# Attention of a hybrid block: head weights half a head ahead, casts of the gated unit's weights behind named exponentials, quotients in halves

## The chip, the cores and the metric

The kernel runs on one core of one Trainium2 chip. The metric is the device time of one execution in microseconds, taken as the median of several runs. A profiled execution of the kernel before, with its trace, serves for the reading.

## The reference

One decoder layer on 1024 tokens of width 1024, in float32. Two branches read the same normalised input `u`: a diagonal state-space branch and a forgetting attention with 8 heads of 64. They are gated and added, projected, and followed by a cross-attention into 256 memory tokens, a gated feed-forward layer and a final norm. Cut to the parts that matter here:

```python
proj = u @ w_in[l]
u_ssm, q, k, v, f_logit, gate_logits = jnp.split(proj, [...], axis=-1)
y_ssm = gelu(s5_ssm(u_ssm, ...))
glu_a, glu_b = jnp.split(y_ssm @ w_glu[l], 2, axis=-1)
out_a = glu_a * sigmoid(glu_b)

# forgetting attention, per head, cum = cumsum(log_sigmoid(f_logit + b_forget))
s = (q @ k.T) * 64 ** -0.5 + cum[:, None] - cum[None, :]
s = where(causal, s, -inf)
att = softmax(s) @ v
out_b = att @ w_fox_o[l]

h = h + (gate_a * out_a + gate_b * out_b) @ w_mix_out[l]
...                      # cross-attention, gated feed-forward, final norm
```

## The kernel before

Products are made to float32's precision from two rounded halves: an operand is split into a high part (a cast on ScalarE, line 178) and a low part (a subtraction on VectorE, line 179), and each product is three matmuls (lines 168 to 170). Weights come through SP's DMA queue into tiles `raw` (two slots), and their halves lie in `whi` and `wlo` (four slots each).

The attention is the class `Fox`. Its loop `run` goes over the heads h = 0 to 7, and within a head over 12 units (qc, kt): a block of 512 queries against a tile of 128 keys, 4 units for the first block of queries and 8 for the second. For a unit, `scores` makes two matmuls (lines 1620 and 1621), adds the causal mask on VectorE (1623), takes the exponential on ScalarE (1627) and splits it into `ph` and `pl`; in four of the units the cast is on VectorE (1629, kept as `self.mark`) and the subtraction on GpSimd (1630), else on ScalarE and VectorE (1632, 1633). `values_hi` follows two units later (1645, 1646), `values_lo` one more unit later (1652). The last exponential that has been written down is `self.exp`.

Beside the units of head h the lists `side[i]`, one for each unit, hold work for later heads:

- the row maxima of head h + 1 (`row_max`, lines 1593 to 1598), turned into one row by `max_row` (1605 to 1610), which a DMA puts into the score operand `hb`;
- the projection of q and k of head h + 2: `parts` (16 steps of three matmuls), and `evac`, which writes the score operands and calls `gate_rows` for the rows of cumulated logs (1575, 1576);
- the split of the weights of head h + 3 at unit 9, and their load at unit 5 (1540, 1541), which is queued behind `self.spread`;
- in head 6 the loads of y, the gated unit's input (1698), into tiles that the normalised input leaves; in head 7 the loads of the finished heads (1704) and `filler`, the value half of the gated unit for its first four column blocks: for each a load with its split (`Glu.load`) and two products (`Glu.value`, each 12 matmuls and a copy on VectorE, line 1087).

When a head's last values are done, `finish` fetches the row of sums over a DMA, takes the reciprocal, writes it out (1665) and spreads it over 64 rows with a third DMA (1667, `self.spread`). `divide` of the head before runs at unit 4: it multiplies the 64 rows (1673), splits the product with lines 178 and 179 into `ahi` and `alo`, and stores both (1679; the last two heads go straight into the operand of the output projection, 1684).

The order in which this is written is not the order on the engines. A planner goes through all instructions with a model of their times and gives every engine and SP's queue a fixed order: it takes what is ready by its model, the one written first if several are, and a tile's slot must have been left by its last user. `tc.issue_after(ins)` binds the instructions that are written within it, and that belong to the engine of `ins`, to places behind `ins` in that engine's order; no wait comes of it. On the chip each engine goes through its list in order and waits at each instruction for what it needs. So a load of the gated unit's weights, written in head 7, can be issued in head 4, and its cast as well.

Of the kernel before, what the change touches and what calls it, by code (L numbers as in the profile page):

```python
# [10 lines left out]
F32R = mybir.dt.float32r  # L11
# [9 lines left out]
D = 1024  # L21
L = 1024
NT = 8
GRP = 32
NH = 8
DH = 64
# [40 lines left out]
def f32(ap):  # L67
    return ap.bitcast(F32)


class Act:


    def __init__(self, pool, tag, bufs, nk, n, kg=2, name="a"):
        self.kg, self.width = kg, D // kg

        def mk(s):
            return [[pool.tile([P, D], F32R, tag=tag, bufs=bufs, name=f"{name}{s}{k}_{h}")
                     .rearrange("p (k c) -> p k c", k=kg)
                     for h in range(n // self.width)] for k in range(nk // kg)]  # L80

        self.hi, self.lo = mk("h"), mk("l")
# [209 lines left out]
@with_exitstack  # L292
def hybrid_block_kernel(ctx: ExitStack, tc: tile.TileContext, x, mem, norm_mix, w_in, b_forget,
                        lam_re, lam_im, log_dt, b_re, b_im, c_re, c_im, d_skip, w_glu, w_fox_o,
                        w_mix_out, norm_mem_q, norm_mem_kv, w_mem_q, w_mem_kv, w_mem_o, norm_ffn,
                        w_ffn_in, w_ffn_out, norm_final, out):
    B = Block(ctx, tc)
    nc, V, A, G, T, S = B.nc, B.V, B.A, B.G, B.T, B.S
    small, const, ident = B.small, B.const, B.ident
    x, mem, out = x[0], mem[0], out[0]  # L300
    w_in, w_glu, w_fox_o, w_mix_out = w_in[0], w_glu[0], w_fox_o[0], w_mix_out[0]
    w_mem_q, w_mem_kv, w_mem_o = w_mem_q[0], w_mem_kv[0], w_mem_o[0]
    w_ffn_in, w_ffn_out = w_ffn_in[0], w_ffn_out[0]

    u_d = B.dram.tile([4, 8, P, P], F32, name="u_d")
    y_d = B.dram.tile([4, 2, 8, P, P], F32, name="y_d")
    gate_d = B.dram.tile([2 * D, L], F32, name="gate_d")
    att_d = B.dram.tile([2, NH * DH, L], F32, name="att_d")
    cum_d = B.dram.tile([NH, 2, L], F32, name="cum_d")
    rd_d = B.dram.tile([NH, L], F32, name="rd_d")  # L310
    kv_d = B.dram.tile([4, P, D], F32, name="kv_d")

    big = ctx.enter_context(tc.tile_pool(name="big", bufs=16))
    uT = Act(big, "big", 16, 8, L, name="u")
    with tc.tile_pool(name="ssm", bufs=1) as sp:
        s5 = S5(B, sp, lam_re[0], lam_im[0], log_dt[0], b_re[0], b_im[0], c_re[0], c_im[0], d_skip[0])
        with tc.tile_pool(name="xin", bufs=1) as xp:
            stage_in(B, xp, s5, x, mem, norm_mix[0], norm_mem_kv[0], w_in, w_mem_kv, uT, u_d, kv_d)
        with tc.tile_pool(name="qp", bufs=1, reuse_waits="tile") as qp:
            stage_ssm(B, s5, qp, uT, w_in, gate_d, u_d, y_d)  # L320
    yT = Act(big, "big", 16, 4, L, name="y")
    aT = Act(big, "big", 16, 4, L, name="at")
    sh = Shared(ctx.enter_context(tc.tile_pool(name="sh", bufs=1, reuse_waits="tile")))
    wg_d = B.dram.tile([4, P, 2 * D], F32, name="wg_d")
    glu = Glu(B, sh, yT, wg_d, gate_d)
    with tc.tile_pool(name="fox", bufs=1, reuse_waits="tile") as fp:
        Fox(B, fp, sh, uT, w_in, b_forget[0], cum_d, rd_d, att_d).run(y_d, yT, aT, w_glu, wg_d,
                                                                       [f for j in range(4) for f in glu.values(j)])
    with tc.tile_pool(name="st2", bufs=1, reuse_waits="tile") as s2:
        stage_tail(B, big, s2, sh, x, glu, aT, gate_d, kv_d, w_fox_o, w_mix_out, norm_mem_q[0], w_mem_q,  # L330
                   w_mem_o, norm_ffn[0], w_ffn_in, w_ffn_out, norm_final, out)
# [732 lines left out]
class Glu:  # L1064


    def __init__(self, B, sh, yT, w_glu, gate_d):
        self.B, self.sh, self.yT, self.w_glu, self.gate_d = B, sh, yT, w_glu, gate_d
        self.w, self.out = {}, {}

    def load(self, j):
        pieces = [(512 * i, (4, P), self.w_glu[:, :, i * D + j * P:i * D + (j + 1) * P].rearrange("k p c -> p k c"))
                  for i in range(2)]
        self.w[j] = [t[:, :D].rearrange("p (k c) -> p k c", k=8) for t in self.B.wload(pieces, D)]

    def product(self, j, h, b):
        ps = self.B.bank("mm" if b == 0 else None)
# [341 lines left out]
class Fox:  # L1419
# [247 lines left out]
        self.spread = S.dma_start(rb, self.rd_d[h].partition_broadcast(64))  # L1667
        self.rb[h] = rb

    def divide(self, h):  # L1670
        B, S = self.B, self.B.S
        num, rb = self.num.pop(h), self.rb.pop(h)
        B.V.tensor_mul(num[0:64, :], num[0:64, :], rb)
        hi = self.fp.tile([64, L], F32R, tag="rb", bufs=2, name="ahi")
        lo = self.fp.tile([64, L], F32R, tag="rb", bufs=2, name="alo")
        B.split(hi, lo, num[0:64, :])
        if h < NH - 2:
            for i, a in enumerate((hi, lo)):
                S.dma_start(self.att_d[i, h * DH:(h + 1) * DH, :], f32(a))
        else:  # L1680
            r = slice((h % 2) * DH, (h % 2 + 1) * DH)
            for hf in range(2):
                for dst, a in zip(self.aT.rhs(h // 2, hf), (hi, lo)):
                    S.dma_start(f32(dst[r, :]), f32(a[:, 512 * hf:512 * hf + 512]))

    def run(self, y_d, yT, aT, w_glu, w_d, filler):
        B, fp, S = self.B, self.fp, self.B.S
        self.aT = aT
        self.prepare_v()
# [5 lines left out]
        def load_y(k, h):  # L1695

            for i, dst in enumerate(yT.rhs(k, h)):
                S.dma_start(f32(dst).rearrange("p (t c) -> p t c", t=4),
                            y_d[k, i, 4 * h:4 * h + 4].rearrange("t p c -> p t c"))

        def load_att(k):
            for h in range(2):
                for i, dst in enumerate(aT.rhs(k, h)):
                    S.dma_start(f32(dst), self.att_d[i, k * P:(k + 1) * P, 512 * h:512 * h + 512])

        pro = [self.project(h) for h in range(NH)]
# [21 lines left out]
        pro[2].load()  # L1728
        pro[2].split(copied)
        pro[3].load()  # L1730
        for t in range(5, 7):
            self.values_of_v(0, t)
        units = [(qc, kt) for qc in range(2) for kt in range(4 * qc + 4)]
        for h in range(NH):
            side = {i: [] for i in range(12)}
            late = h == NH - 2
            if late:
                for i, f in enumerate(pro[h + 1].parts[8:]):
                    side[i // 2].append(f)
                side[3].append(pro[h + 1].evac[1])  # L1740
            if h + 1 < NH:
                for i, f in enumerate(self.row_max(h + 1)):
                    side[(RSLOT_LATE if late else RSLOT)[i]].append(f)
                side[9].append(lambda: self.max_row(h + 1))
            if h + 2 < NH:
                n = 8 if h + 3 == NH else 16
                for i, f in enumerate(pro[h + 2].parts[:n]):
                    side[i if n == 8 else PSLOT[i]].append(f)
                side[9].append(pro[h + 2].evac[0])
                if n == 16:  # L1750
                    side[11].append(pro[h + 2].evac[1])
            if h + 3 < NH:
                side[9].append(lambda: pro[h + 3].split(self.exp))
            if h > 0 and h + 3 < NH:
                side[5].append(lambda: pro[h + 3].load(self.spread))
            if h == 0:
                side[0].append(lambda: self.values_of_v(0, 7))
            if late:
                for k in range(8):
                    side[4 + k].append(lambda k=k: load_y(k // 2, k % 2))  # L1760
            if h == NH - 1:
                for k in range(3):
                    side[6 + k].append(lambda k=k: load_att(k))
                for i, f in enumerate(filler):
                    side[i * 12 // len(filler)].append(f)
            for i, u in enumerate(units):
                self.scores(h, *u)
                for f in side[i]:
                    f()
                if len(self.hi_todo) > 2:  # L1770
                    self.values_hi()
                if len(self.lo_todo) > 1:
                    self.values_lo()
                if h and i == 4:
                    with B.tc.issue_after(self.mark.ins):
                        self.divide(h - 1)
        while self.hi_todo:
            self.values_hi()
        while self.lo_todo:
            self.values_lo()  # L1780
        self.divide(NH - 1)


_INS = ["x", "mem", "norm_mix", "w_in", "b_forget", "lam_re", "lam_im", "log_dt", "b_re", "b_im", "c_re", "c_im",
# [26 lines left out]
```

## Time and profile before

| what | value |
|---|---|
| median of 3 runs | 1591.73 us (1591.47 to 1593.48) |
| profiled execution, span from its first to its last instruction | 1586.7 us |
| median of the runs less that span | 5.03 us |
| TensorE matmul busy, granted clock over the span | 1534.0 us (97%), 0.988 |
| weight load busy | 1261.3 us (79%) |
| VectorE, ScalarE, GpSimd busy | 1019.5, 655.2, 254.3 us |
| heads 1, 2, 3 (first exponential to the next head's) | about 24.75 us each |
| first exponential of head 4, of head 5, of head 6, of head 7 | 499.36, 529.83, 553.42, 579.40 us |

For the profiled execution the profile gives the span and no other time, so the span is what stands beside the runs. In the rows of the trace the first figure is the start in us from the span's start, the second the duration in us, then engine, line, operation and operands; in square brackets stands how long the engine was idle before it, and what ended the wait. `SPq` is the issue of a DMA on SP's queue, not its transfer. In rows of stretches each engine has its busy time with the count of instructions behind it.

### The profile page before, as it was taken

Reading aid. Unit: us, or ns where it says so; the run is one execution under the profiler, and the core shown is the slowest. Engines: PE = TensorE matmul, PEld = TensorE weight load, DVE = VectorE, ACT = ScalarE, POOL = GpSimd, SP = SyncE. Lnnn points to the kernel's source line nnn. Section 1 sums busy time; section 2 is a strip of 40 time slices with the busy share of each in tenths; the row PEclk is TensorE's granted clock in tenths of the full one; section 3 lists DMA queues with packets and bytes.
Section 4 is the critical chain, followed back from the end, with each engine's and each line's share of the span. In section 5 each row is a group of like instructions: output and inputs, shape, how many; then the busy total and the mean of one; then the engine's idle time right before and its main releaser. Section 6 shows DMA issues by size and latency. Waiting matters only on the chain.

```text
span 1586.7 us, 20446 instructions
## 1 busy us (share of the span) xinstructions
PE 1534.0 (97%) x7313; PEld 1261.3 (79%) x7313; DVE 1019.5 (64%) x1850; ACT 655.2 (41%) x1173; POOL 254.3 (16%) x335
## 2 busy tenths in 40 slices
PE   7799999999999899999999999999999999999997
PEld 6578888898777668888888778888888888788885
DVE  6666445344688687675555697766677776565555
ACT  6422434323576553222435564333333333254342
POOL 2027653200212124110002200100000000000001
PEclk8899999999999999999999999999999999999999
DMA  7764445652023736357412186555444554796642
GB/s 266 125 132 80 127 131 110 130 145 30 18 52 48 186 95 208 125 172 259 160 46 75 54 283 239 170 164 163 155 153 160 166 162 156 261 391 223 195 150 106
DMA packets 197940, 240.86 MB, mean 152 GB/s; under 512 B 35448, under 2 KB 126488, under 8 KB 197328
## 3 DMA queue, kind: packets, MB, share of 16 engines
q1 hardware_dynamic: 191216, 223.84, 48.2%
q10 hardware_dynamic: 6624, 15.73, 2.6%
q8 instruction: 57, 0.93, 0.2%
q14 instruction: 43, 0.35, 0.1%
HBM read 165.60 MB, written 75.86 MB: 152 GB/s over the span
## 4 chain that ended last, share of the span: by engine, by line
PE 75%; DVE 8%; DMA 7%; issue 4%; POOL 3%; ACT 2%; SPq 1%; DVEq 0%; POOLq 0%; ACTq 0%
PE mm L868 14%; PE mm L168 7%; PE pv L868 7%; PE mm L170 7%; PE mm L169 7%; PE mm L1005 4%; PE sc L868 3%; PE sc L1005 3%; PE pv L1005 3%; PE sc L168 3%; PE sc L169 3%; PE sc L170 3%; DMA raw<-in_w_in_dram 2%; PE misc L1005 1%; PE pv L168 1%
## 5 line engine op out<-in xcount | busy, mean ns | idle before, releaser
L179 DVE TENSOR_TENSOR wlo<-raw,whi 128x1024 fp32r<-128x1024 f32 (+2 forms) x121 | 132.0, 1094 | 135.1 <-ACT whi L178 133.9
L178 ACT CAST whi<-raw 128x1024 fp32r<-128x1024 f32 (+2 forms) x124 | 116.1, 940 | 220.0 <-DMA raw<-in_w_ffn_in_dram 54.1
L168 PE MATMUL mm<-uh,whi 128*128 128x512 f32 x344 | 138.8, 404 | 2.8 <-ACT whi L178 2.7
L170 PE MATMUL mm<-uh,wlo 128*128 128x512 f32 x344 | 136.5, 397 | 1.7 <-DVE wlo L179 1.7
L169 PE MATMUL mm<-ul,whi 128*128 128x512 f32 x344 | 136.4, 396 | 0.0
L179 DVE TENSOR_TENSOR ol<-or,oh 128x1024 fp32r<-128x1024 f32 x73 | 89.3, 1224 | 71.6 <-ACT oh L178 70.3
L178 ACT CAST oh<-or 128x1024 fp32r<-128x1024 f32 x73 | 76.8, 1052 | 105.3 <-PE mm L1005 33.6
L900 POOL TENSOR_TENSOR g<-a,c 128x512 f32<-128x512 f32 x22 | 35.2, 1600 | 392.8 <-ACT a L899 373.9
L170 PEld LDWEIGHTS mm<-uh,wlo 128*128 128x128 f32 x344 | 65.7, 191 | 16.5 <-DVE wlo L179 3.1
L1630 POOL TENSOR_TENSOR pl<-pf,ph 128x512 fp32r<-128x512 f32 (+1 forms) x32 | 39.7, 1239 | 241.1 <-DVE ph L1629 196.1
L168 PEld LDWEIGHTS mm<-uh,whi 128*128 128x128 f32 x344 | 65.9, 192 | 15.5 <-ACT whi L178 3.2
L169 PEld LDWEIGHTS mm<-ul,whi 128*128 128x128 f32 x344 | 66.0, 192 | 11.3
L197 POOL TENSOR_TENSOR r<-ms,mhalf 128x1 f32<-128x1 f32 x26 | 15.1, 582 | 354.9 <-DVE ms L193 344.5
L1627 ACT ACTIVATE pf<-sc 128x512 f32<-128x512 f32 (+1 forms) x96 | 46.5, 490 | 46.3 <-DVE sc L1623 28.6
L868 PE MATMUL pv<-S3h,we 128*128 128x512 f32 x176 | 58.1, 389 | 0.0
L1633 DVE TENSOR_TENSOR pl<-pf,ph 128x512 fp32r<-128x512 f32 (+2 forms) x64 | 35.1, 550 | 10.2 <-ACT ph L1632 9.5
L1005 PE MATMUL mm<-oh 128*128 128x512 f32 x106 | 41.2, 389 | 0.0
L1005 PE MATMUL mm<-ol,oh 128*128 128x512 f32 x106 | 41.2, 389 | 0.0
L1005 PE MATMUL mm<-oh,ol 128*128 128x512 f32 x106 | 41.2, 389 | 0.0
L168 PE MATMUL mm<-yh,whi 128*128 128x512 f32 x104 | 40.9, 393 | 0.0
L168 PE MATMUL sc<-uh,whi 128*128 128x512 f32 x104 | 40.8, 393 | 0.0
L170 PE MATMUL mm<-yh,wlo 128*128 128x512 f32 x104 | 40.6, 390 | 0.0
(580 smaller groups left out, 4537.5 us busy)
## 6 DMA issues: line engine op xcount, KB each, us to landing
or<-c_d SPq DMA_DIRECT2D x77, 256.0 KB
raw<-in_w_in_dram SPq DMA_DIRECT2D x22, 512.0 KB
wo<-in_w_ffn_out_dram SPq DMA_DIRECT2D x22, 512.0 KB
c_d<-g SPq DMA_DIRECT2D x44, 256.0 KB
t_d<-wo SPq DMA_DIRECT2D x44, 256.0 KB
or<-t_d SPq DMA_DIRECT2D x44, 256.0 KB
raw<-in_w_ffn_in_dram SPq DMA_DIRECT2D x20, 512.0 KB
rawb<-in_w_ffn_in_dram SPq DMA_DIRECT2D x20, 512.0 KB
```

The source lines that it names most:

```text
L168: T.matmul(ps, lh, rh, start=first, stop=False)
L169: T.matmul(ps, lh, rl, start=False, stop=False)
L170: T.matmul(ps, ll, rh, start=False, stop=last)
L178: self.A.copy(hi, src)
L179: (self.G if pool_lo else self.V).tensor_sub(lo, src, f32(hi))
L197: self.G.tensor_tensor(out=r, in0=v, in1=self.mhalf[:, 0:n], op=ALU.pow)
L868: T.matmul(ps, l_[:, k, :], r_, start=first and k == 0 and i == 0, stop=k == 3 and i == 2, skip_group_check=True)
L900: G.tensor_mul(g[:, 512:], a1, c1)
L1005: T.matmul(ps, l_[:, gi], r_[:, 512:], start=n < 3 and p == 0 and k == 0 or n == 7 and p == 0 and k == 0, stop=p == NP - 1 and k == 2, ski ...
L1627: self.exp = A.activation(pf[:, off:], ps[:, off:], AF.Exp)
L1630: G.tensor_sub(pl[:, off:], pf[:, off:], f32(ph[:, off:]))
L1633: V.tensor_sub(pl[:, off:], pf[:, off:], f32(ph[:, off:]))
```

## The change

Three things are changed, all in the attention.

- Head weights: the load of head h + 4 is written at unit 7 of head h (for head 0 too), where the load of head h + 3 was at unit 5 of heads 1 to 4. It is queued behind the spread of the head before, in head 0 behind an exponential. The splits stay at unit 9 for head h + 3.
- The gated unit's weights: the list of loads and products is moved one unit up: the first load stands at unit 10 of head 6, the other 11 steps at units 0 to 10 of head 7. The cast of each load is bound to come behind the exponential that was written last, on ScalarE's queue.
- `divide` is cut in two: at unit 4 the whole product and the split of the first 512 columns, at unit 6 the split of the second 512, bound behind that unit's exponential. The last two heads store each half as it is done, the others both at the end.

```diff
--- before.py
+++ after.py
@@ -324,8 +324,7 @@
     wg_d = B.dram.tile([4, P, 2 * D], F32, name="wg_d")
     glu = Glu(B, sh, yT, wg_d, gate_d)
     with tc.tile_pool(name="fox", bufs=1, reuse_waits="tile") as fp:
-        Fox(B, fp, sh, uT, w_in, b_forget[0], cum_d, rd_d, att_d).run(y_d, yT, aT, w_glu, wg_d,
-                                                                       [f for j in range(4) for f in glu.values(j)])
+        Fox(B, fp, sh, uT, w_in, b_forget[0], cum_d, rd_d, att_d).run(y_d, yT, aT, w_glu, wg_d, glu)
     with tc.tile_pool(name="st2", bufs=1, reuse_waits="tile") as s2:
         stage_tail(B, big, s2, sh, x, glu, aT, gate_d, kv_d, w_fox_o, w_mix_out, norm_mem_q[0], w_mem_q,
                    w_mem_o, norm_ffn[0], w_ffn_in, w_ffn_out, norm_final, out)
@@ -1067,11 +1066,12 @@
     def __init__(self, B, sh, yT, w_glu, gate_d):
         self.B, self.sh, self.yT, self.w_glu, self.gate_d = B, sh, yT, w_glu, gate_d
         self.w, self.out = {}, {}
+        self.after = None
 
     def load(self, j):
         pieces = [(512 * i, (4, P), self.w_glu[:, :, i * D + j * P:i * D + (j + 1) * P].rearrange("k p c -> p k c"))
                   for i in range(2)]
-        self.w[j] = [t[:, :D].rearrange("p (k c) -> p k c", k=8) for t in self.B.wload(pieces, D)]
+        self.w[j] = [t[:, :D].rearrange("p (k c) -> p k c", k=8) for t in self.B.wload(pieces, D, behind=self.after)]
 
     def product(self, j, h, b):
         ps = self.B.bank("mm" if b == 0 else None)
@@ -1667,23 +1667,23 @@
         self.spread = S.dma_start(rb, self.rd_d[h].partition_broadcast(64))
         self.rb[h] = rb
 
-    def divide(self, h):
+    def divide(self, h, hf):
         B, S = self.B, self.B.S
-        num, rb = self.num.pop(h), self.rb.pop(h)
-        B.V.tensor_mul(num[0:64, :], num[0:64, :], rb)
-        hi = self.fp.tile([64, L], F32R, tag="rb", bufs=2, name="ahi")
-        lo = self.fp.tile([64, L], F32R, tag="rb", bufs=2, name="alo")
-        B.split(hi, lo, num[0:64, :])
-        if h < NH - 2:
-            for i, a in enumerate((hi, lo)):
+        num = self.num[h]
+        cs = slice(512 * hf, 512 * hf + 512)
+        if hf == 0:
+            B.V.tensor_mul(num[0:64, :], num[0:64, :], self.rb.pop(h))
+            self.att = [self.fp.tile([64, L], F32R, tag="rb", bufs=2, name=n) for n in ("ahi", "alo")]
+        B.split(*[a[:, cs] for a in self.att], num[0:64, cs])
+        if h >= NH - 2:
+            r = slice((h % 2) * DH, (h % 2 + 1) * DH)
+            for dst, a in zip(self.aT.rhs(h // 2, hf), self.att):
+                S.dma_start(f32(dst[r, :]), f32(a[:, cs]))
+        elif hf:
+            for i, a in enumerate(self.att):
                 S.dma_start(self.att_d[i, h * DH:(h + 1) * DH, :], f32(a))
-        else:
-            r = slice((h % 2) * DH, (h % 2 + 1) * DH)
-            for hf in range(2):
-                for dst, a in zip(self.aT.rhs(h // 2, hf), (hi, lo)):
-                    S.dma_start(f32(dst[r, :]), f32(a[:, 512 * hf:512 * hf + 512]))
-
-    def run(self, y_d, yT, aT, w_glu, w_d, filler):
+
+    def run(self, y_d, yT, aT, w_glu, w_d, glu):
         B, fp, S = self.B, self.fp, self.B.S
         self.aT = aT
         self.prepare_v()
@@ -1728,6 +1728,13 @@
         pro[2].load()
         pro[2].split(copied)
         pro[3].load()
+        gated = [f for j in range(4) for f in glu.values(j)]
+
+        def behind_exp(f):
+            glu.after = self.exp
+            f()
+            glu.after = None
+
         for t in range(5, 7):
             self.values_of_v(0, t)
         units = [(qc, kt) for qc in range(2) for kt in range(4 * qc + 4)]
@@ -1751,18 +1758,19 @@
                     side[11].append(pro[h + 2].evac[1])
             if h + 3 < NH:
                 side[9].append(lambda: pro[h + 3].split(self.exp))
-            if h > 0 and h + 3 < NH:
-                side[5].append(lambda: pro[h + 3].load(self.spread))
+            if h + 4 < NH:
+                side[7].append(lambda: pro[h + 4].load(self.spread if h else self.exp))
             if h == 0:
                 side[0].append(lambda: self.values_of_v(0, 7))
             if late:
                 for k in range(8):
                     side[4 + k].append(lambda k=k: load_y(k // 2, k % 2))
+                side[10].append(lambda: behind_exp(gated[0]))
             if h == NH - 1:
                 for k in range(3):
                     side[6 + k].append(lambda k=k: load_att(k))
-                for i, f in enumerate(filler):
-                    side[i * 12 // len(filler)].append(f)
+                for i, f in enumerate(gated[1:]):
+                    side[i].append(lambda f=f: behind_exp(f))
             for i, u in enumerate(units):
                 self.scores(h, *u)
                 for f in side[i]:
@@ -1771,14 +1779,15 @@
                     self.values_hi()
                 if len(self.lo_todo) > 1:
                     self.values_lo()
-                if h and i == 4:
-                    with B.tc.issue_after(self.mark.ins):
-                        self.divide(h - 1)
+                if h and i in (4, 6):
+                    with B.tc.issue_after(self.mark.ins if i == 4 else self.exp.ins):
+                        self.divide(h - 1, i // 2 - 2)
         while self.hi_todo:
             self.values_hi()
         while self.lo_todo:
             self.values_lo()
-        self.divide(NH - 1)
+        for hf in range(2):
+            self.divide(NH - 1, hf)
 
 
 _INS = ["x", "mem", "norm_mix", "w_in", "b_forget", "lam_re", "lam_im", "log_dt", "b_re", "b_im", "c_re", "c_im",
```

## The prediction

> **What bounds the kernel now.** I read the page first, then each engine's busy time cut at the first exponential of each attention head, then the instructions of the heads in which TensorE stops.
>
> ```profile
> span 1586.7 us, 20446 instructions
> PE 1534.0 (97%) x7313; PEld 1261.3 (79%) x7313; DVE 1019.5 (64%) x1850; ACT 655.2 (41%) x1173; POOL 254.3 (16%) x335
> ```
>
> TensorE is busy for 97% of the span: only about 53 us of gaps exist, and the change touches only those of the attention heads. In the stretches below the columns are length, busy time and instructions of PE, PEld, DVE, ACT and POOL, then granted TensorE clock, DMA share and GB/s.
>
> ```profile
> 474.20:499.00 24.80, 24.76 (x122) 18.85 (x122) 20.27 (x51) 16.77 (x32) 4.60 (x4) 1.00 0.33 55
> 499.00:529.45 30.45, 26.95 (x122) 19.66 (x122) 21.34 (x51) 17.84 (x34) 4.60 (x4) 0.94 0.39 79
> 529.45:553.00 23.55, 21.52 (x107) 15.77 (x106) 18.48 (x51) 13.39 (x27) 4.62 (x4) 1.00 0.89 227
> 553.00:579.00 26.00, 22.66 (x107) 15.55 (x106) 22.15 (x48) 16.45 (x31) 6.37 (x4) 1.00 0.41 110
> 579.00:605.60 26.60, 26.52 (x129) 20.68 (x128) 17.34 (x29) 10.94 (x23) 4.63 (x4) 1.00 0.47 139
> 600.00:800.00 200.00, 200.00 (x901) 165.66 (x900) 131.65 (x173) 63.46 (x109) 31.60 (x22) 1.00 0.54 176
> ```
>
> These are heads 3 to 7 and the 200 us from 600 on. Head 3 is filled by TensorE (24.76 of 24.80 us). Head 4 has the same 122 matmuls and takes 30.45 us, 5.65 more: 3.50 is TensorE idle, 1.8 is clock (0.06 of 30.45), 0.3 I leave unplaced. Heads 5, 6 and 7 have 2.03, 3.34 and 0.08 us of idle. From 600 us TensorE has no gap, so I let what the heads save reach the end in full. All of it together is 5.65 + 2.03 + 3.34 + 0.08 = 11.1 us.
>
> **Head weights one head earlier.** Here is what stops head 4: ACT's casts, TensorE's wait, the clock after it, the DMA queue.
>
> ```profile
> 521.54 1.04 ACT L178 CAST whi<-raw 128x1024 fp32r<-128x1024 f32 x1 [4.85 <-DMA raw<-in_w_in_dram]
> 523.18 1.05 ACT L178 CAST whi<-raw 128x1024 fp32r<-128x1024 f32 x1 [0.18 <-DMA raw<-wg_d]
> 522.64 0.50 PE L168 MATMUL mm<-uh,whi 128*128 128x512 f32 x1 [2.74 <-ACT whi L178]
> 526.00:528.00 2.00, 2.00 (x8) 1.50 (x7) 1.70 (x4) 0.22 (x1) 0.00 (x0) 0.50 0.26 78
> 431.27 0.57 SPq L1540 DMA_DIRECT2D raw<-in_w_in_dram  x1
> 442.00:444.00 2.00, 2.00 (x11) 1.39 (x12) 1.97 (x5) 1.86 (x4) 0.40 (x1) 1.00 0.00 0
> 480.36 0.58 SPq L1540 DMA_DIRECT2D raw<-in_w_in_dram  x1
> 505.17 0.58 SPq L1540 DMA_DIRECT2D raw<-in_w_in_dram  x1
> 506.42 8.55 SPq L153 DMA_DIRECT2D raw<-wg_d  x2
> 508.00:510.00 2.00, 2.00 (x12) 1.50 (x11) 1.83 (x4) 0.93 (x2) 0.00 (x0) 1.00 0.45 26
> ```
>
> Head 1's load is issued at 431.27 and the DMA engines are empty by 442: about 10 us, and its cast comes later than that. In head 4 the load of head 7's weights (505.17) is followed at once by the first load of the gated unit's weights (506.42), whose issue holds SP's queue for 8.55 us while the engines move 26 GB/s. The head's weights are there only at 521.5, 16 us after their issue. ACT, in order, waits 4.85 us with the exponentials of units 10 and 11 behind it, and TensorE waits 2.74 us, then runs at half clock (0.50).
>
> The change issues each of heads 4 to 7's loads behind the spread of the head before, where a load goes today, but for the next head. Head 7's goes out near 480.4 and its cast stays near 516: 36 us for a 10 us transfer. Neither slot of `raw` is then free for the gated unit until head 6's weights are split at about 494, so the two loads no longer meet. Head 4's extra load is issued in head 0, where nothing else is to be moved:
>
> ```profile
> 380.00:420.00 40.00, 40.00 (x220) 32.39 (x219) 26.16 (x71) 18.98 (x36) 4.62 (x4) 1.00 0.00 1
> ```
>
> Its pin to an exponential orders nothing, since `issue_after` binds only instructions of the named one's engine and the load is SP's; at 1 GB/s that costs 0. Value: head 4 becomes head 3, **-5.65 us**; at worst the wait goes and half returns, -2.8. The lost clock in it is a measured 1.8 us. The Trainium skill, "TensorE: Matmul & The Clock Gate", section "Why this matters for your kernels", asks for idle gaps above about 3 us before the clock drops; here a gap of 2.74 us was followed by 0.50, so the trace is stricter. By the page no clock would have been lost to this gap, and the term would be about -3.8.
>
> **Gated unit's first transfers, now ahead of the rows of maxima.** Their casts are pinned, not their transfers. The first one takes the slot that head 6's weights leave:
>
> ```profile
> 493.12 1.22 DVE L179 TENSOR_TENSOR wlo<-raw,whi 128x1024 fp32r<-128x1024 f32 x1
> 494.56 0.70 SPq L1610 DMA_DIRECT2D hb<-mr  x1
> 498.36 0.39 PE L1620 MATMUL sc<-hb 69*128 69x512 f32 x1
> 503.14 0.35 SPq L1665 DMA_DIRECT2D rd_d<-rc  x1
> 504.65 0.47 SPq L1667 DMA_DIRECT2D rb<-rd_d  x1
> 548.81 2.08 SPq L153 DMA_DIRECT2D raw<-wg_d  x4
> 550.00:552.00 2.00, 1.97 (x12) 1.43 (x13) 1.15 (x4) 1.27 (x4) 0.00 (x0) 1.00 0.95 277
> 552.00:554.00 2.00, 2.00 (x11) 1.52 (x9) 0.85 (x3) 0.58 (x2) 0.00 (x0) 1.00 0.86 241
> ```
>
> The subtraction ends at 494.34, and head 4's row of maxima is issued at 494.56 and needed at 498.36. Two issues of 2.08 / 4 = 0.52 us get in between, and 0.5 MB at about 260 GB/s is 2.0 us, beginning some 1.2 us after its issue: drained at 494.34 + 1.2 + 2.0 = 497.5. A small transfer takes 1.5 us (503.14 to 504.65, where the second waits for the first). So the row lands near 498, just in time; the same comes at the end of head 4 with the second transfer. Lower end 0, upper end as under the rivals; I take **+0.5 us** for both.
>
> **Head 5.** Its wait is of another kind:
>
> ```profile
> 541.53 1.22 DVE L1673 TENSOR_TENSOR num<-num,rb 64x1024 f32<-64x1024 f32 x1 [1.60 <-DMA rb<-rd_d]
> 544.50 0.39 PE L1620 MATMUL sc<-hb,hb 69*128 69x256 f32 x1 [1.51 <-ACT pf L1627]
> ```
>
> The reciprocals of head 4 come late behind the loads of y, which the change leaves alone, and the product that waits for them stays whole. **0**; ends -2.03 (all of the idle gone, as ACT waits half as long for the shorter subtraction) and +0.5.
>
> **Head 6: the casts leave, and so does the filler.**
>
> ```profile
> 555.28 1.05 ACT L178 CAST whi<-raw 128x1024 fp32r<-128x1024 f32 x1
> 556.79 0.39 PE L1645 MATMUL pv<-ph,vhi 128*65 128x384 f32 x1 [0.60 <-ACT ph L1632]
> 558.00 1.04 ACT L178 CAST whi<-raw 128x1024 fp32r<-128x1024 f32 x1
> 559.39 0.51 PE L1620 MATMUL sc<-hb 69*128 69x512 f32 x1 [0.45 <-ACT pf L1627]
> 553.00:579.00 26.00, 6.13 (x18) 3.38 (x18) 0.00 (x0) 0.00 (x0) 1.00 0.41 110
> 553.00:579.00 26.00, 3.53 (x9) 1.69 (x9) 0.00 (x0) 1.00 0.41 110
> 575.88 2.19 DVE L1087 COPY sg<-mm 128x512 f32<-128x512 f32 x2
> ```
>
> Two casts inside head 6 each cost TensorE a wait (0.60 and 0.45). But because the weights are split so early, 18 + 9 = 27 matmuls of the gated unit (the two rows by tile, those that read y's high and low parts) run in head 6 and fill it. At 200 us / 901 = 0.222 us each they are 6.0 us. After the change the first cast follows the exponential of unit 10, so most of them move to head 7. Head 6 keeps 22.66 - 6.0 = 16.7 us of TensorE work; VectorE keeps 22.15 - 3 x 1.22 - 2.19 = 16.3, and 1.22 for the one subtraction, 17.5. No shorter than 17.5, then: idle 0.9, a change of -2.5. Head 5 with nearly that VectorE work ran 23.55 - 18.48 = 5.1 us over it: 22.6, idle 5.9, **+2.6**. The middle, 20.05, has 3.4 of idle, as now: **0**. I take the middle because the first products can still start within the head, in the gap after unit 10.
>
> **Head 7.** Three casts (3 x 1.05 on ACT) and three subtractions (3 x 1.22 on VectorE) enter it. It has 26.52 us of TensorE work, with the moved products some 32, against ACT's 10.94 and VectorE's 17.34: room for all. Each cast stands ahead of an exponential's own cast on ACT, so a wait like head 6's is possible: 0 to 3 x 0.6 = 1.8; I take **+0.8**. The next transfer starts when a cast frees its slot and has three units to land; two pairs took until 554 from 548.81, 5 us.
>
> **Quotients in halves.** A 64x1024 cast and subtraction become two of half the width, and the second cast follows the exponential of unit 6, by when VectorE is done with the first. Heads 1 to 4 hide the few tenths behind TensorE's 24.8; the copy of the next quotient, which waits for the last subtraction to leave `num`, is not needed before the bank comes round a head later. **0**, ends -0.5 and +0.5.
>
> **Sum.** -5.65 + 0.5 + 0 + 0 + 0.8 + 0 = -4.35 us on the profiled execution's span: 1582.35. The median of the runs, 1591.73, stands 5.03 above that span; what lies around it does not change: **1587.4**.
>
> **Rivals.** *Given back in heads 6 and 7.* Head 4's gain comes, but the missing filler costs the 2.6 and the casts the 1.8: -5.65 + 0.5 + 2.6 + 1.8 = -0.75, time 1591.0. For it speaks that head 6 loses 6 us of independent work; against it that VectorE's own load falls from 22.15 to 17.5. Chance 0.18, and with it 0.03 that the planner again puts a gated transfer beside a head's load, or that other waits come up, and nothing moves (1591.7).
>
> *Slower: the row of maxima behind the gated transfer.* Place: SP's queue at the end of heads 3 and 4. If the transfer moves as it did after 506.42 (26 GB/s) rather than as after 548.81, the row lands many microseconds late; all 12 scores of the next head wait, and TensorE stops long enough for the clock to drop. The point is a delay above 498.36 - 494.56 - 1.5 = 2.3 us. Price: twice a stop like head 4's, 2 x 5.65, in place of the 0.5: 1587.4 - 0.5 + 11.3 = 1598.2. Against it: the slow case had another load of narrow rows ahead of it, the fast one had not. Chance 0.17. The Trainium skill, "DMA: Bandwidth & Descriptors", section "Queues, rings and completion order", says that an engine takes the descriptors of one ring in order, which is what this rival needs; no row of this trace has a row of maxima directly behind a gated load.
>
> **Numbers.** The forecast has 0.62; its own range is 1582 to 1590. The lower ends, -5.65 - 2.03 - 2.5 for heads 4 to 6 and 0 for the rest, give -10.2 and 1581.5. The upper ends without the slow rival end at 1591.0 + 0.5 + 0.5 = 1592.0; with one of its two stops and the forecast's other terms, 1592.6. To leave out no more than 2 in 10 I go to 1596, between one stop and two. What a measurement of this kernel can tell from no change is about 0.2%, 3.2 us. Faster by more: 0.56 (the forecast less the part above 1588.5); within: 0.24 (that part, the first rival, one stop); slower: 0.20.
>
> **What would show it.** Right: the stretch of head 4 shrinks to about 25 us with a clock of 1.00, and no cast waits for w_in. No gated matmul before head 6's unit 10, and all of the rest in head 7, longer than now by some 5 us. Wrong: a wait of TensorE for the score operands right at the start of head 4 or 5 (the slower rival), head 6 no shorter than 26 us less the moved 6, plus 2 or more of idle (the first rival), or a cast on ACT in head 7 that waits for wg_d. Gaps in the tail that the before kernel lacks would break the carrying over.

## The result: 0.44% slower

| kernel | median of the runs | ratio to the kernel before |
|---|---|---|
| before | 1591.91 us (1587.22 to 1593.48) | 1 |
| changed | 1599.53 us (1597.31 to 1600.83) | 1.0044 [1.0032, 1.0056] |

The forecast was 1587.4 us with a range up to 1596.0. The time lies above the range, on the other side, and not by the mechanism of the slower rival. The profiled execution of the changed kernel took 1597.31 us, 1.7 more than its span, so the 5.03 us that the prediction put around the span of before were mostly the spread between executions.

The page of the changed kernel, and its stretches between the first exponentials of heads 1 to 7, of the stage's end (616.56, the load of the sigmoid's table) and of what follows:

```profile
span 1595.6 us, 20478 instructions
PE 1536.5 (96%) x7313; PEld 1263.5 (79%) x7313; DVE 1022.5 (64%) x1858; ACT 656.1 (41%) x1181; POOL 253.7 (16%) x335
```
```profile
425.16:451.61 26.45, 25.48 (x124) 19.07 (x122) 21.02 (x53) 16.90 (x33) 5.51 (x4) 1.00 0.25 52
451.61:477.95 26.34, 25.17 (x121) 18.96 (x121) 20.88 (x54) 16.79 (x33) 5.52 (x4) 1.00 0.31 52
477.95:504.26 26.31, 24.73 (x117) 18.44 (x118) 20.62 (x52) 16.79 (x33) 5.52 (x4) 1.00 0.37 71
504.26:530.61 26.35, 25.67 (x127) 19.24 (x125) 21.09 (x53) 16.79 (x33) 5.52 (x4) 1.00 0.18 46
530.61:555.19 24.58, 20.78 (x101) 15.12 (x102) 18.40 (x49) 13.61 (x29) 4.59 (x4) 1.00 0.80 209
555.19:579.75 24.56, 19.30 (x83) 13.60 (x83) 18.17 (x45) 14.83 (x30) 4.60 (x4) 0.86 0.23 55
579.75:616.56 36.81, 34.64 (x161) 25.75 (x160) 23.91 (x35) 14.86 (x28) 4.99 (x4) 1.00 0.53 151
616.56:800.00 183.44, 183.44 (x815) 152.01 (x814) 120.67 (x157) 58.05 (x93) 29.17 (x21) 1.00 0.57 185
```

TensorE's busy time has grown by 2.5 us for the same number of matmuls. From the sigmoid's table to the end the changed kernel takes 979.0 us and the kernel before 980.5, so what the heads lose reaches the end. The same cuts in the kernels of the experiments give this table (us, one profiled execution each). The ratios are against runs of the kernel before on the same chip, whose median lay between 1590.6 and 1592.7 us.

| kernel | heads 1 to 3 | head 4 | head 5 | heads 6 and 7 | ratio of the medians |
|---|---|---|---|---|---|
| before | 75.7 | 30.5 | 23.6 | 52.8 | 1 |
| **changed** | **79.1** | **26.4** | **24.6** | **61.4** | **1.0044** |
| loads alone | 75.6 | 25.0 | 23.3 | 52.8 | 0.9971 |
| casts alone | 75.7 | 29.1 | 24.0 | 59.1 | 1.0030 |
| halves alone | 79.3 | 31.4 | 23.6 | 53.5 | 1.0036 |
| loads and casts | 75.6 | 24.7 | 25.4 | 59.1 | 1.0000 |
| loads, steps unbound | 75.7 | 25.0 | 24.1 | 53.1 | 0.9954 |
| loads, first cast at unit 6 | 75.7 | 24.7 | 23.7 | 56.3 | 0.9978 |
| loads, first cast alone bound | 75.7 | 24.7 | 23.9 | 55.5 | 0.9980 |
| loads, whole quotient at unit 6 | 75.7 | 25.1 | 25.4 | 52.0 | 0.9957 |
| quotient's casts in halves | 77.0 | 30.0 | 23.7 | 53.7 | 0.9996 |
| quotient's subtractions in halves | 76.2 | 32.4 | 24.2 | 52.1 | 1.0004 |

The changed kernel wins 4.1 us in head 4, loses 3.4 in heads 1 to 3, 1.0 in head 5 and 8.6 in heads 6 and 7: +8.9 us, as much as the two spans differ (1.5 us more ahead of head 1 and 1.5 less behind head 7 cancel). Heads 1, 2 and 3 of the kernel before last 26.1, 24.8 and 24.8 us; "about 24.75" in the table of the time before holds for heads 2 and 3 only. The 1.0 of head 5 is no more than two executions of one kernel differ there (24.1 and 25.1 us with the loads and the steps unbound). Two places carry the loss.

**Each head's start.** TensorE (first two rows) and ScalarE at the start of head 3:

```profile
477.41 0.22 PE L1593 MATMUL mm<-hb 68*128 68x128 f32 x1
478.60 0.38 PE L1620 MATMUL sc<-hb,hb 69*128 69x256 f32 x1 [0.97 <-ACT pf L1627]
477.35 0.58 ACT L1568 CAST hb<-mm 64x512 fp32r<-64x512 f32 x1
477.95 0.60 ACT L1627 ACTIVATE pf<-sc 128x512 f32<-128x512 f32 x1
```

The score of the third unit (256 columns) waits 0.97 us for the head's first exponential, which stands on ScalarE behind a cast of the score operands. Nothing else stands ahead of that score in TensorE's list; the next matmul starts at 478.82.

**Head 6.** TensorE, then what it waits for on VectorE and ScalarE, then the clock:

```profile
568.01 0.40 PE L1652 MATMUL pv<-pl,vhi 128*65 128x512 f32 x1
573.45 0.37 PE L1607 MATMUL misc<-ident,mc 128*8 128x128 f32 x1 [5.04 <-DVE mc L1605]
568.21 1.22 DVE L1675 TENSOR_TENSOR num<-num,rb 64x1024 f32<-64x1024 f32 x1 [1.45 <-DMA rb<-rd_d]
569.46 1.14 ACT L178 CAST ahi<-num 64x512 fp32r<-64x512 f32 x2 [3.54 <-DVE num L1675]
570.43 1.28 DVE L179 TENSOR_TENSOR alo<-num,ahi 64x512 fp32r<-64x512 f32 x2
573.25 0.15 DVE L1605 TENSOR_TENSOR mc<-mc 128x8 f32<-128x8 f32 x1
```
```profile
572.00:574.00 2.00, 0.50 (x2) 0.21 (x2) 1.47 (x7) 1.10 (x3) 0.00 (x0) 0.50 0.94 201
576.00:578.00 2.00, 2.00 (x8) 1.48 (x8) 1.73 (x4) 0.66 (x2) 0.00 (x0) 0.50 0.00 0
```

The transposition of head 7's row maxima (line 1607) waits 5.04 us for VectorE, which starts the quotient at 568.21, behind a wait of 1.45 us for the spread reciprocals, and does its halves in between; no other work stands ahead of line 1607 in TensorE's list. Then TensorE runs at half clock until about 579. In the kernel with the loads alone the same place is covered. Here are the last matmul ahead of the stop, the first of the gated unit, the transposition without any wait, and what VectorE does meanwhile:

```profile
563.04 0.40 PE L1652 MATMUL pv<-pl,vhi 128*65 128x512 f32 x1
563.37 0.50 PE L168 MATMUL mm<-yh,whi 128*128 128x512 f32 x1
...
566.90 0.27 PE L1607 MATMUL misc<-ident,mc 128*8 128x128 f32 x1
566.59 0.15 DVE L1605 TENSOR_TENSOR mc<-mc 128x8 f32<-128x8 f32 x1
```

From 563.37 to 566.90 fifteen matmuls of the gated unit stand in TensorE's list, 3.5 us; in the changed kernel's list none is left ahead of line 1607.

### The profile page after: what moved, and what is told of

Same layout as the page of the kernel before. It is cut to its first block, busy times and chain, and to the rows that moved or that the text cites. A ratio compares the mean times of both kernels' runs of the same rounds, so it can differ in the third digit from the quotient of the medians.

```text
span 1595.6 us, 20478 instructions
## 1 busy us (share of the span) xinstructions
PE 1536.5 (96%) x7313; PEld 1263.5 (79%) x7313; DVE 1022.5 (64%) x1858; ACT 656.1 (41%) x1181; POOL 253.7 (16%) x335
## 4 chain that ended last, share of the span: by engine, by line
PE 71%; DVE 11%; DMA 6%; issue 5%; ACT 4%; POOL 3%; SPq 1%; DVEq 0%; POOLq 0%; ACTq 0%
PE mm L867 14%; PE pv L867 7%; PE mm L170 6%; PE mm L168 6%; PE mm L169 6%; PE mm L1004 5%; PE sc L1004 4%; PE sc L867 3%; PE pv L1004 3%; PE sc L168 3%; PE sc L169 3%; PE sc L170 3%; DMA raw<-in_w_in_dram 2%; PE misc L1004 2%; PE pv L168 1%
```

## The experiments

### One part at a time

Each part of the change by itself on the kernel before, and two of them together. The edits are the parts of the diff shown above.

**Loads alone**

```diff
-            if h > 0 and h + 3 < NH:
-                side[5].append(lambda: pro[h + 3].load(self.spread))
+            if h + 4 < NH:
+                side[7].append(lambda: pro[h + 4].load(self.spread if h else self.exp))
```

> The kernel before with only the head weights loaded one head earlier. The planner's lists of TensorE, VectorE, ScalarE and GpSimd stay as before; only SP's list changes. Theory (the transfer behind the gated one is what stops head 4, and nothing else hangs on it): head 4 falls from 30.4 to about 24.8 us, no idle before the cast of head 7's weights, the other heads as before; 1591.9 - 5.6 = 1586.3. Rival (the early loads are what makes heads 1 to 4 of the changed kernel 1.5 us longer each, by their transfers): heads 2 and 3 at 26.3 us instead of 24.8 and no gain over the whole, 1591 or more.

1586.84 us, 0.9971 [0.9959, 0.9983]. Heads 4 to 7:

```profile
501.59:526.59 25.00, 24.97 (x124) 19.02 (x124) 21.50 (x52) 17.75 (x34) 4.60 (x4) 1.00 0.22 54
526.59:549.89 23.30, 21.34 (x106) 15.55 (x104) 18.20 (x51) 13.25 (x27) 4.62 (x4) 1.00 0.89 236
549.89:575.88 25.99, 22.67 (x106) 15.60 (x105) 22.37 (x48) 16.58 (x31) 6.35 (x4) 1.00 0.38 106
575.88:602.71 26.83, 26.75 (x129) 20.79 (x129) 17.06 (x28) 11.38 (x23) 4.62 (x4) 1.00 0.46 138
```

Head 4 is 25.00 us at full clock where it was 30.5: the stop is gone, and nothing is given back in heads 5 to 7. On TensorE, VectorE, ScalarE and GpSimd the planner's lists are those of before; only SP's differs.

**Casts alone**

```diff
-    ...run(y_d, yT, aT, w_glu, wg_d, [f for j in range(4) for f in glu.values(j)])
+    ...run(y_d, yT, aT, w_glu, wg_d, glu)
...
+                side[10].append(lambda: behind_exp(gated[0]))
...
-                for i, f in enumerate(filler):
-                    side[i * 12 // len(filler)].append(f)
+                for i, f in enumerate(gated[1:]):
+                    side[i].append(lambda f=f: behind_exp(f))
```

> The kernel before with only the gated unit's steps one unit up and its casts bound behind exponentials. Theory (the filler that leaves head 6 is what the 5 us wait there costs): head 4 keeps its 30 us stall, heads 1 to 3 stay at 24.8, head 6 gets a wait of TensorE for the row maxima of about 5 us with the clock at a half after it, and the products move to head 7: 4 to 8 us slower, 1596 to 1600. Rival (the wait in head 6 comes from the halves, which put the whole product and two subtractions ahead of the last row maxima on VectorE): no wait over 2 us in head 6, within 2 us of before, 1590 to 1594.

1596.15 us, 1.0030 [1.0018, 1.0042]. Heads 6 and 7 last 59.1 us instead of 52.8:

```profile
551.32:573.89 22.57, 18.71 (x78) 12.60 (x77) 18.53 (x44) 14.51 (x28) 4.59 (x4) 0.85 0.26 68
573.89:610.39 36.50, 34.22 (x159) 25.41 (x158) 23.56 (x33) 14.78 (x28) 4.62 (x4) 1.00 0.50 147
```

Head 6 has lost 28 matmuls, keeps 3.9 us of idle and runs at a mean clock of 0.85; head 7 has 30 more and is 9.7 us longer. The stop at line 1607 is 3.7 us here, where about 5 was expected.

**Halves alone**

```diff
-                if h and i == 4:
-                    with B.tc.issue_after(self.mark.ins):
-                        self.divide(h - 1)
+                if h and i in (4, 6):
+                    with B.tc.issue_after(self.mark.ins if i == 4 else self.exp.ins):
+                        self.divide(h - 1, i // 2 - 2)
```

> The kernel before with only the quotients split in halves. Theory (the halves turn the planner's order of heads 1 to 4 into one that leaves TensorE waiting): heads 2 and 3 at 26.3 us instead of 24.8, in all 5 to 6 us slower by heads 1 to 4, less what of head 4's stall the longer heads take up, so 1592 to 1598. Rival (the early loads do that): heads 2 and 3 stay at 24.8, within 2 us of before, 1590 to 1594.

1596.40 us, 1.0036 [1.0022, 1.0051]. Heads 2 and 3 last 26.33 and 26.30 us, 1.5 more than in the kernel before; head 1 is 0.5 longer and head 4, with its stop still there, 1.0. This is head 3:

```profile
476.48:502.78 26.30, 25.15 (x121) 18.96 (x121) 20.81 (x54) 16.79 (x33) 5.50 (x4) 1.00 0.30 52
```

**Loads and casts**, the change without the halves:

> The changed kernel without the halves. Theory: head 4 at 24.8, heads 2 and 3 at 24.8, the wait in head 6 stays: the loads' gain of 5.6 against the casts' loss of 4 to 8, 1590 to 1594. Rival (the halves make the wait in head 6): the wait is gone as well, 1586 or less.

1591.39 us, 1.0000 [0.9986, 1.0014]. The gain of the loads and the cost of the casts cancel. The single effects, -4.6, +4.8 and +5.7 us by the ratios, add to +5.9, and the whole change costs +7.0 (5.1 to 8.9): an effect of the parts on each other is not shown.

### Why the halves cost 1.5 us in heads 2 and 3

The place of the second half is not it. Written at unit 6 and bound to the mark instead of the exponential, it gets lists that are the same on all five queues; written at unit 4, lists that differ in the order of two stores of the last heads. So the cut is left. What was open was whether it is the time of the smaller instructions or the other order that the planner writes around them.

**Only the cast in halves**

```diff
-        B.split(hi, lo, num[0:64, :])
+        for hf in range(2):
+            cs = slice(512 * hf, 512 * hf + 512)
+            B.A.copy(hi[:, cs], num[0:64, cs])
+        B.V.tensor_sub(lo, num[0:64, :], f32(hi))
```

> The kernel before, with only ScalarE's cast of the quotient cut in two halves (ahi, line 178); VectorE's subtraction stays whole, in its old place. TensorE's list through heads 1 to 6 is that of before but for one place. Theory 'order': what costs about 1.5 us in each of heads 1 to 4 with halves of both is the other order in which the planner then writes the heads, not the extra instruction. Then heads 2 and 3 last 24.8 us here as before, and the whole is within 0.2% of before (1587.5 to 1593.5 us). Rival 'small instructions': two halves take longer than one whole (1.14 against 1.05 us on ScalarE, 1.62 against 1.22 us on VectorE), and this delays the exponentials that follow on the same engine. Then heads 2 and 3 are longer here too, by a share of the 1.5 us, some 0.3 us each.

**Only the subtraction in halves**

```diff
-        B.split(hi, lo, num[0:64, :])
+        B.A.copy(hi, num[0:64, :])
+        for hf in range(2):
+            cs = slice(512 * hf, 512 * hf + 512)
+            B.V.tensor_sub(lo[:, cs], num[0:64, cs], f32(hi[:, cs]))
```

> The kernel before, with only VectorE's subtraction of the quotient cut in two halves (alo, line 179); the cast stays whole. TensorE's list departs from that of before from head 1 on. Theory 'order': heads 1 to 4 then leave 24.8 us, most likely for about 26.3 us as with halves of both, and the whole is 1595 to 1597 us. Rival 'small instructions': 0.4 us more on VectorE in each head, which has 4 us idle in each, so that heads 2 and 3 become longer by 0 to 0.4 us, and the whole is 1590 to 1593 us.

1590.87 us, 0.9996 [0.9985, 1.0006], and 1593.09 us, 1.0004 [0.9995, 1.0014]. Head 2 with the casts in halves, then with the subtractions:

```profile
454.08:478.89 24.81, 24.77 (x123) 18.87 (x123) 20.23 (x51) 16.86 (x34) 4.61 (x4) 1.00 0.27 55
```
```profile
451.30:476.39 25.09, 25.08 (x122) 18.83 (x121) 20.01 (x52) 16.38 (x32) 4.64 (x4) 1.00 0.28 54
```

Neither theory came through whole. The casts alone cost heads 2 and 3 nothing, as "order" said; TensorE's list through heads 1 to 4 is that of before. The subtractions alone change TensorE's list from head 1 on and cost 0.3 us a head, which is what "small instructions" allowed and not the 1.5 that "order" expected. So another order is not dear in every case. But the two together cost 1.5, so 1.2 us of it appears with neither cut alone.

The traces show what is different in the list with both cuts. The quotient's two casts still run back to back, at the place of the whole one in ScalarE's list, so the cut spreads nothing. On VectorE the planner puts a step in writing the score operands of a later head (line 1564) behind the quotient's subtractions, 16.2 us into head 2, where it stood ahead of them, at 11.5 us. The later steps of these operands follow late, and head 3's first exponential stands on ScalarE behind the last of them. TensorE's first score, on the other hand, comes 3.4 us ahead of that exponential (at 476.48) instead of 1.0 (at 476.80). Here is the halves alone, TensorE at the start of head 3, then VectorE in head 2; then the same rows of the loads alone:

```profile
473.07 0.40 PE L1620 MATMUL sc<-hb,hb 69*128 69x512 f32 x1
477.13 0.39 PE L1620 MATMUL sc<-hb,hb 69*128 69x256 f32 x1 [0.96 <-ACT pf L1627]
462.83 1.62 DVE L179 TENSOR_TENSOR alo<-num,ahi 64x512 fp32r<-64x512 f32 x2
466.35 0.68 DVE L1564 SCALAR_TENSOR_TENSOR hb<-mm,hb 64x512 fp32r<-64x512 f32 x1
```
```profile
475.80 0.40 PE L1620 MATMUL sc<-hb,hb 69*128 69x512 f32 x1
477.45 0.39 PE L1620 MATMUL sc<-hb,hb 69*128 69x256 f32 x1
463.51 0.68 DVE L1564 SCALAR_TENSOR_TENSOR hb<-mm,hb 64x512 fp32r<-64x512 f32 x1
464.22 1.22 DVE L179 TENSOR_TENSOR alo<-num,ahi 64x1024 fp32r<-64x1024 f32 x1
```

This chain and its wait of 0.96 us are read from the traces; no run isolated them, so that the order is the cause is argued, and some 0.5 of the 1.5 us is left unplaced. Head 1 with the casts in halves, 27.4 us against 26.1, has a stop of its own (1.24 us on TensorE) and shows that even the smaller cut is not free everywhere.

**The whole quotient at unit 6**, on top of the loads:

```diff
-                if h and i == 4:
+                if h and i == 6:
```

> Head weights loaded earlier; the quotient whole, written at unit 6 in place of unit 4. TensorE's list is that of the loads alone through heads 1 to 5, with 17 matmuls of the gated unit ahead of line 1607 in place of 15. Theory 'the cut, not the place': heads 2 and 3 last 24.8 us, and the whole is that of the loads alone within 0.2% (1584 to 1589 us). Rival 'the place': the later quotient takes VectorE and ScalarE where the exponentials need them, heads 1 to 4 go to 26 us as with the halves, and the whole is 1591 us or more.

1587.11 us, 0.9957 [0.9942, 0.9972]; head 2 lasts 24.86 us. The later place of the whole quotient costs nothing; the cut does.

### Why the casts cost 6 us in heads 6 and 7

**Steps one unit up, casts not bound**

```diff
         def behind_exp(f):
-            glu.after = self.exp
+            glu.after = None
             f()
```

> Head weights loaded earlier and the gated unit's steps written one unit up, as in the kernel with both parts (1591.4 us), but the casts of the gated unit's weights not bound behind exponentials. Theory 'binding': the binding holds the first cast back to unit 10 of head 6 and with it every product that could fill head 6. Without it 15 matmuls of the gated unit stand ahead of the transposition of head 7's row maxima on TensorE (line 1607) as in the kernel before, where the binding leaves none; the wait of 3.7 us there is gone, heads 6 and 7 together last 52.8 us where they lasted 59.1, and the whole is 1586 to 1588 us, as with the loads alone. Rival 'place': the loads written one unit up meet other transfers, and the cost stays: 1590 to 1592 us.

1585.25 us, 0.9954 [0.9941, 0.9966]; heads 6 and 7 last 53.1 us, without the wait at line 1607:

```profile
548.76:574.76 26.00, 22.63 (x106) 15.59 (x105) 22.37 (x48) 16.60 (x32) 6.36 (x4) 1.00 0.39 107
574.76:601.87 27.11, 26.94 (x130) 20.79 (x130) 16.95 (x28) 11.49 (x23) 4.61 (x4) 1.00 0.46 137
```

The binding is the cause, as its theory said. The place of the steps is nothing: with the first load written at unit 4, 6, 8 or 10 of head 6 and no binding, the lists are the same. Run once more beside the loads alone:

> Head weights loaded earlier and the gated unit's steps one unit up, the casts not bound. Theory 'no effect of the place': what the planner can move freely it puts where it was, 15 matmuls of the gated unit ahead of line 1607 in head 6 with the steps either way, so the time is that of the loads alone within 0.2% (3 us). Rival 'a gain of its own': the steps one unit up are worth the 1.6 us that lay between the two kernels in separate comparisons (1585.3 and 1586.8 us), and it lies 1 to 2 us below the loads alone here too.

> Head weights loaded earlier and nothing else, beside the kernel with the steps unbound. Both theories: 0.997 of before, some 4.6 us less.

1586.54 us, 0.9962 [0.9948, 0.9977], and 1586.48 us, 0.9965 [0.9952, 0.9978]. No gain of its own.

**First cast four units earlier, all bound**

```diff
-                side[10].append(lambda: behind_exp(gated[0]))
+                side[6].append(lambda: behind_exp(gated[0]))
```

> As the kernel with both parts (1591.4 us), all casts bound, but the first load written at unit 6 of head 6 in place of unit 10, so that its cast is bound behind the exponential of unit 6. Theory 'filler': it is the first cast alone that empties head 6. With it four units earlier 18 matmuls of the gated unit stand ahead of line 1607 in head 6, the wait of 3.7 us and the half clock behind it go, and heads 6 and 7 together last 53 to 55 us: 1585 to 1588 us. Rival 'all casts': the other three casts, bound to units 2, 5 and 8 of head 7, keep the products for the end of head 7, which stays near 36 us less what moved; heads 6 and 7 last 57 us or more and the whole 1589 to 1591 us.

1589.37 us, 0.9978 [0.9965, 0.9990]; heads 6 and 7 last 56.3 us, between both theories, and the whole lies where "all casts" had it. The wait at line 1607 is gone; what is left is in head 7, with waits of TensorE for the casts and subtractions of the gated unit. The list of its waits from 545 to 612 us (total, times, longest) has, among others:

```profile
PE mm L170 <- DVE wlo L179: 1.5, 2, 0.9
PE mm L168 <- ACT whi L178: 0.4, 1, 0.4
```

**First cast alone bound**

```diff
-                    side[i].append(lambda f=f: behind_exp(f))
+                    side[i].append(f)
```

> As the kernel with loads and casts (1591.4 us, heads 6 and 7 together 59.1 us), but only the first cast is bound, behind the exponential of unit 10 in head 6; the other three are free. With the first cast four units earlier and all four bound, heads 6 and 7 lasted 56.3 us; with none bound 53.1 us. Theory 'two halves': the first binding empties head 6 (no matmul of the gated unit ahead of line 1607, a wait of 3.7 us there, half clock behind it), the other three make TensorE wait for casts in head 7. Then heads 6 and 7 last 55.5 to 57 us here, with the wait at line 1607 and without the waits for line 178 in head 7, and the whole is 1588 to 1590 us. Rival 'the first alone': everything queues behind the first cast, so heads 6 and 7 last 58.5 to 59.5 us, and the whole is 1590.5 to 1592 us.

1588.81 us, 0.9980 [0.9968, 0.9992]; heads 6 and 7 last 55.45 us. TensorE's stop, then heads 6 and 7:

```profile
565.07 0.38 PE L1607 MATMUL misc<-ident,mc 128*8 128x128 f32 x1 [3.69 <-DVE mc L1605]
```
```profile
549.36:572.22 22.86, 19.00 (x78) 12.81 (x77) 19.56 (x45) 15.46 (x29) 4.59 (x4) 0.85 0.28 70
572.22:604.81 32.59, 32.42 (x159) 25.62 (x158) 21.31 (x32) 14.29 (x27) 5.52 (x4) 1.00 0.53 163
```

"Two halves" holds, at its lower end: the first binding costs 2.6 us (55.45 less the 52.8 of the loads alone), the other three another 3.7 (59.1 with all). In the 2.6 idle time counts little: it is 3.9 + 0.2 us in heads 6 and 7, against 3.3 + 0.1 with the loads alone, since the moved products fill head 7. The busy time has grown by 2.0 us, from 49.4 to 51.4 (two more matmuls on record make up some 0.4), with a mean clock of 0.85 in head 6. So the stop cost mostly by the half clock behind it, which the rows of this one execution show.

## Why the prediction was wrong, point by point

- **Head weights, -5.65: right.** With the loads alone head 4 became 25.00 us at a clock of 1.00, in the changed kernel no cast on ScalarE waits for a DMA in the attention any more, and the run of that part alone gave -4.6 us (-2.7 to -6.5 by its interval), and -5.6 in the second comparison.
- **First transfers ahead of the rows of maxima, +0.5: the order was wrong, and the size was near by luck.** The transfers are issued behind those rows, as SP's rows at the end of head 3 show:

```profile
497.73 0.70 SPq L1610 DMA_DIRECT2D hb<-mr  x1
...
499.36 0.93 SPq L153 DMA_DIRECT2D raw<-wg_d  x2
501.77 0.47 PE L1620 MATMUL sc<-hb 69*128 69x512 f32 x1 [0.74 <-DMA hb<-mr]
```

  TensorE waits 0.74 us for the row at one head and not at all at the next. With the loads alone the transfers go out behind the row too (498.01 behind 496.76), and TensorE does not wait for it, so the 0.74 is not shown to be theirs. The slower rival, built on that order, did not occur.
- **Head 5, 0 with ends -2.03 and +0.5:** +1.0 in the changed kernel, above its upper end, and -0.3 with the loads alone. In other runs it lay between 23.3 and 25.4; see the last section.
- **Head 6, 0 with the upper end +2.6, and head 7, +0.8: mis-sized, and the first step that failed.** The step is "I take the middle because the first products can still start within the head, in the gap after unit 10". They did start there (7 in the changed kernel, the first at 577.13), but behind the stop. The prediction weighed VectorE's load and did not ask what TensorE's list would hold while VectorE did the quotient and the last row maxima. It held nothing: 3.7 us of stop in the kernels with casts and whole quotients, 5.04 with halves, and half clock behind it, which the sum had at nothing. Together the two heads lengthened by 6.3 us by the casts where +0.8 stood, and by 8.6 with the halves. Of the 6.3, loads and casts against the loads alone, 0.5 is more idle time in head 6, 2.2 more idle in head 7 and 3.6 more busy time. The first rival, "given back in heads 6 and 7", had 4.4 for this and was nearest for the casts; of the price it left out the busy time. What it said would show it, a head 6 with 2 us or more of idle, is there (24.56 - 19.30 = 5.3 us). TensorE also waits for the later casts and subtractions in head 7 (1.4 us in the changed kernel), but none of these casts waits for `wg_d`. By the measured +4.8 and -4.6, loads and casts come to that rival's "nothing gained".
- **Quotients in halves, 0 with ends -0.5 and +0.5: the second step that failed.** "Heads 1 to 4 hide the few tenths behind TensorE's 24.8" priced the instructions, and each of them cut alone does cost only 0 to 0.3 us in heads 2 and 3. It took the rest of the list as given. It also had VectorE done with the first half before the second half's cast; in head 2 of the changed kernel the two casts run back to back (463.65 and 464.17), ahead of both subtractions (from 464.30). The planner wrote the heads in another order from head 1 on, and each of the heads 2 and 3 became 26.3 us: +5.7 us in the whole, over ten times the upper end.
- **Carried to the end: right.** The row behind "from 600 us TensorE has no gap" ends at 800 us; from there to 1590 TensorE is busy for 767.9 of 790 us. Even so the rest took 979.0 us where it had taken 980.5.
- **The way it went.** The sum of the two failed terms, +4.8 + 5.7, against the one that held, -4.6, is +5.9 where -4.35 was forecast. No rival put a price on the order itself, so the range ended at 1596.0.

Of the kernels run, those with the loads and without binding or halves are faster than the kernel before and the changed one: 0.9954 to 0.9971 of the kernel before in five comparisons, whose intervals overlap, so none of the three is shown to be the best.

## What to carry to other kernels

Where a planner orders instructions, an edit's price is not the time of its instructions: in heads where TensorE was busy for 24.76 of 24.80 us, a quotient with one instruction cut in halves cost 0 to 0.3 us, and with both cut, in another order, 1.5. Before work is bound to a later place, find the longest stretch in which its consumer's list would then be empty: here fifteen products, 3.5 us, were all that hid a chain of another engine. An earlier load, with no instruction of the engines reordered, gave -4.6 and -5.6 us in two comparisons, where -5.65 was forecast.

## What was not expected of the hardware

The clock after a short stop of TensorE is not set by the length of the stop alone. In head 5 the same score waits for the same exponential in the kernel with the steps unbound (second run; with the clock of a stretch behind it) and in the loads alone (second run; likewise):

```profile
541.41 0.39 PE L1620 MATMUL sc<-hb,hb 69*128 69x256 f32 x1 [1.92 <-ACT pf L1627]
542.00:544.00 2.00, 2.00 (x6) 1.42 (x6) 1.97 (x7) 1.17 (x3) 1.28 (x1) 0.50 0.88 202
```
```profile
542.24 0.39 PE L1620 MATMUL sc<-hb,hb 69*128 69x256 f32 x1 [2.12 <-ACT pf L1627]
544.00:546.00 2.00, 2.00 (x13) 1.50 (x12) 1.91 (x5) 1.01 (x2) 0.73 (x1) 1.00 0.83 195
```

A wait of 1.92 us was followed by half clock, one of 2.12 us by full clock; in the first case head 5 lasted 25.12 us, in the second 24.22. The gap of 2.74 us in head 4 of the kernel before, on which the prediction rests a comparison, was not alone: the granted clock stayed at 1.00 for some 2 us behind it, with two more waits of 0.53 and 0.19 us, and fell to 0.50 then. So what the one gap did is not shown.

The stops of 3.69 and 5.04 us had half clock behind them, and the single wait of 0.97 us at a head's start had not. Several short ones close together did it too: with the first cast at unit 6, TensorE was busy for 0.71 of 2 us at the start of head 7, with no wait above 0.81 us, and then slow:

```profile
572.00:574.00 2.00, 0.71 (x6) 0.31 (x3) 0.82 (x4) 1.64 (x4) 0.00 (x0) 1.00 0.00 0
574.00:576.00 2.00, 2.00 (x7) 1.52 (x8) 1.76 (x5) 1.97 (x5) 0.19 (x1) 0.53 0.03 2
```

The Trainium skill, "TensorE: Matmul & The Clock Gate", section "What's actually happening", tells of a free-running window of activity of about 3.4 us, so that the slow matmuls vary from run to run; the variation agrees with these rows, while the drop after 1.92 us comes sooner than a whole idle window.
